# Retention's values and gates and the sparse keys and values: projected by seven block products ahead of the attention, and handed over through DRAM

## The chip, the cores and the metric

The kernel is one program on one core of a Trainium2 chip. The metric is the device time in microseconds of one execution, lower is better: the time that the core needs from the start to the end of the program. Everything is float32; TensorE takes its operands as fp32r, in three passes (below).

## The reference, cut to what matters

A decoder trunk of two layers on 512 tokens of width 1024. Each layer is a half SwiGLU block, a mixer and another half SwiGLU block. The mixer normalises `x` to `u`, projects `u` with one matrix `W_in`, splits the columns among four branches and merges the branches under gates:

```python
u = rms_norm(x, mix_norm[l])
(a_q, a_k, a_v, b_x, b_b, b_c,
 c_q, c_kc, c_vc, c_ks, c_vs, c_kw, c_vw, c_g,
 d_q, d_k, d_v, d_g, gate_logits) = jnp.split(u @ w_in[l], SPLIT_POINTS, axis=-1)
y_a = swa_sink_mixer(a_q, a_k, a_v, ...)          # attention in a window of 128
y_b = short_conv_mixer(b_x, b_b, b_c, conv_w[l])
y_c = nsa_mixer(c_q, c_kc, c_vc, c_ks, c_vs, c_kw, c_vw, c_g, ...)
y_d = retention_mixer(d_q, d_k, d_v, d_g, ...)    # silu(gate) * norm(o), o from q, k, v
branch = jnp.einsum('btnw,nwd->btnd', ys, w_branch[l])
merged = jnp.sum(sigmoid(gate_logits + bias) * branch, axis=2)
x = x + merged @ w_out[l]
```

The columns that matter here are three blocks of 512: `d_v` (values of the retention), `d_g` (its gate), and `c_ks, c_vs, c_kw, c_vw` (four blocks of 128: keys and values of the selected and of the windowed attention of branch C; called the sparse keys and values here).

## The kernel before, in words

**A product in three passes.** A factor `x` is split into `hi` (rounded to fp32r, by ScalarE, line 214) and `lo = x - hi` (by VectorE, line 215). A product is `hi*hi + hi*lo + lo*hi`, three matmuls for each tile of 128 rows of the contraction. This split is the work that ScalarE and VectorE do for every weight.

**Seven block products.** The feed-forward blocks and the stage `early` compute a product with a 2x2 block scheme of seven products in place of eight: the contraction (1024) and the 512 tokens are halved, sums of blocks of the weights are formed by VectorE (`sum_t`, line 439), and combinations of the token blocks are kept ready in `Ahi`, `Alo` and `E` (`factor`, line 330). `step` (line 442) makes one such step for 512 columns of weights: seven units `r1, r2, r6, r5, r7, r3, r4`, each of 24 matmuls of 256 columns (`product`, line 426, line 433), with the copies and sums that put the four output blocks into the tile `O`. `step` loads its weights by two transfers of 1 MB (`load_pair`), one step ahead. Output: features on partitions, tokens along the free dimension; the stationary operand is the weight, the moving one the tokens.

**Dense projections.** In the mixer, `proj_fm` (line 763; features on partitions) and `proj_tm` (line 769; tokens on partitions) multiply without the scheme: for 512 columns 96 matmuls of 512 columns (4 token tiles x 8 rows of the contraction x 3 passes), lines 232 and 782. `proj_tm` leaves its result in four PSUM tiles.

**The order of a layer.** `ffn1`; then `early(l)`: the gates of merge 2 (two steps), the convolution (three steps) and half the gates of merges 1 and 0 (two steps), seven steps in all; gates go to DRAM (`gated`), the convolution too (`yconv`). Then `mixer`: `swa_prep`, `swa`, `merge(1)`, `retention`, `merge(0)`, `nsa`, `merge(3)`, `merge(2)`, the product with `w_out`, and `ffn2`. In `retention` (line 848) four dense projections stand in this order: gates and queries (280 columns), keys (256), values `ps_v` (512), gate `ps_g` (512). The queries and keys are rotated by VectorE (lines 881 to 889, eight operations of 256 elements for each of four token tiles); the gate goes through tanh (line 900) and two VectorE operations of 512 (lines 901, 902). Then a loop over four chunks of 128 tokens: transposes (908), scores (924), mask (925), values (931), state (933, 938, 945), statistics and a reciprocal root (949 to 954), scale (958), gate (959), transposes (962), and `put_y` (840), which splits the result for the merge. In `nsa` the query projection comes first, then `proj_tm(O_KS, 512)` with the compression's products between its halves, then `kv_prep` (line 1012), then the attention.

**What sets the order.** A planner puts each engine's instructions into a fixed order ahead of time: program order is the priority, `tc.high_priority()` lifts an instruction, and what is ready fills the gaps. So the matmuls of a merge (line 232 for its gates, line 828 for its branch product) fill TensorE while the attention written before it waits for VectorE. `tc.issue_after(mark["swa"])` keeps retention's matmuls behind the last value matmul of `swa`; `issue_after(mark["ret"])` keeps those of `nsa` behind retention's last matmul of line 933. SP issues the weight loads in its order, POOL (GpSimd's queue) the loads of gates from DRAM (line 796, two buffers `th`).

Of the kernel before, what the change touches and what calls it, by code (L numbers as in the profile page):

```python
# [13 lines left out]
OP = mybir.AluOpType  # L14
# [58 lines left out]
def body(tc, ins, out):  # L73
# [20 lines left out]
    def fv(ap):  # L94
        return ap.bitcast(F32)
# [157 lines left out]
    def leave(key):  # L253
        ph[key + "_cm"].__exit__(None, None, None)
        ph[key] = None

    def open_x():
        fp = enter("fp", "right")
        ph["XT"] = [fp.tile([128, T], F32, name="XT", tag=f"XT{d}", bufs=1) for d in range(KT)]

    def e_t():
        return cp.tile([128, 2048], F32R, name="E", tag="E", bufs=3)
# [157 lines left out]
        act.activation(t, ps, AF.Copy)  # L420
        return t

    def half(t):
        return t.rearrange("p (w t) -> p w t", w=2)

    def product(ps, w, u, first, last):
# [12 lines left out]
        dve.tensor_tensor(t, a, b, op=OP.add)  # L439
        return t  # L440

    def step(line, raws, srcs, p, use, norm=None, between=([], [])):

        v = {}  # L450

        def blocks(p):
            if p not in raws:
                raws[p] = load_pair(*srcs[p])
            v = raws[p].rearrange("p w (c b) (a n) -> p (w c) b a n", b=2, a=2)
            return [[v[:, :, b, a] for b in range(2)] for a in range(2)]
# [24 lines left out]
        def p4():  # L481
            return unit(v["X"][1][1])

        def r1(w):
            v["x"] = sc_t()
            product(v["x"], w, 0, True, False)
            v["sn1"] = snap(v["x"], "sn1")

        def r2(w):
            py = pv_t()  # L490
            product(py, w, 1, True, True)
            v["O"] = ph["hp"].tile([128, 2048], F32, name="O", tag="O", bufs=2).rearrange("p (w f h t) -> p w f h t", w=2, f=2, h=2)
            dve.tensor_tensor(v["O"][:, :, 0, 0], half(py), half(v["sn1"]), op=OP.add)
# [12 lines left out]
        def r7(w):  # L506
            product(v["x"], w, 4, False, False)
            dve.scalar_tensor_tensor(v["O"][:, :, 1, 1], half(v["x"]), -1.0, half(v["Z"]), op0=OP.mult, op1=OP.subtract)

        def r3(w):  # L510
            product(v["z"], w, 5, False, True)
            dve.tensor_tensor(v["O"][:, :, 0, 1], half(v["z"]), half(v["U"]), op=OP.add)

        def r4(w):
            product(v["x"], w, 6, False, True)
            act.activation(v["O"][:, :, 1, 0], half(v["x"]), AF.Copy, scale=-1.0)
# [12 lines left out]
        line.add(p4, r4)  # L529
# [97 lines left out]
    def early(l):  # L627
# [46 lines left out]
        def gate_cols(b, half_):  # L674
            o = O_MG + b * D + half_ * 512
            return [cols(o), cols(o + 256)]

        for q in range(2):
            srcs.append(gate_cols(2, q))
            uses.append(gates(2, q))  # L680
        for q in range(2):
            srcs.append([cols(O_BX + 256 * q), cols(O_BC + 256 * q)])
            uses.append(conv(2 * q))
# [3 lines left out]
            srcs.append(gate_cols(b, 1))  # L687
            uses.append(gates(b, 1))
        for p in range(len(srcs)):
            step(line, raws, srcs, p, uses[p], norm_end if p == 0 else None)  # L690
        return line


    def mixer(l, spill, F):
# [48 lines left out]
        def w2():  # L743
            return mp.tile([128, 512], F32, name="w2", tag="w2", bufs=6)
# [1 line left out]
        def ks_t():  # L746
            return aq.tile([128, 512], F32, name="ks", tag="ks", bufs=2)

        mark, pv_last, scaled = {}, [None], {}

        def together(first, ready):

# [35 lines left out]
        def merge(b, y, perm, done=None):  # L788
# [2 lines left out]
            gen = weights_fm(w_in, O_MG + b * D, KT if (b, 1) not in slots else KT // 2)  # L791

            def gate(d):
                if (b, d // 4) in slots:
# [45 lines left out]
        def put_y(ps, y, i):  # L840

            ts = slice(i * 128, (i + 1) * 128)
            p = ps.rearrange("p (k t) -> p k t", k=4)
            act.activation(y[0][:, :, ts], p, AF.Copy)
            dve.tensor_tensor(y[1][:, :, ts], p, fv(y[0][:, :, ts]), op=OP.subtract)


        def retention(ps_q, ps_k, ps_v, ps_g):

            yh, yl = y_tiles()  # L850
            o_ = 128 + _CM
# [36 lines left out]
                dve.tensor_tensor(t[:, 0:4], rot[:, 0:4], C["xi"][:, :, None].to_broadcast([128, 4, HD]), op=OP.mult)  # L888
                dve.tensor_tensor(t[:, 4:8], rot[:, 4:8], C["zeta"][:, :, None].to_broadcast([128, 4, HD]), op=OP.mult)
            v = [b4().rearrange("p (i e) -> p i e", i=2) for _ in range(2)]  # L890
            pv = ps_v()
            for i in range(NT):
                act.activation(v[i // 2][:, i % 2], pv[i], AF.Copy, scale=rc[:, i:i + 1])
            g = [b4().rearrange("p (i e) -> p i e", i=2) for _ in range(2)]
            pg = ps_g()
            for i in range(NT):
                x = g[i // 2][:, i % 2]
                act.activation(x, pg[i], AF.Copy, scale=rc[:, i:i + 1])
# [113 lines left out]
        def kv_prep(pk, nt, gains):  # L1012
# [3 lines left out]
            m = 2 * nt  # L1016
            ss = small([128, NT * m], name="kss", bufs=2)
            krs = []
            for i in range(NT):
                src = pk[i][:, :256 * nt].rearrange("p (y w n) -> p y w n", y=nt, w=2)  # L1020
                act.activation(Vt[:, i], src[:, :, 1], AF.Copy, scale=rc[:, i:i + 1])
                kr = w2()[:, :128 * nt].rearrange("p (y n) -> p y n", y=nt)
                act.activation(kr, src[:, :, 0], AF.Copy, scale=rc[:, i:i + 1])
# [173 lines left out]
        def nsa(gates):  # L1197
# [1 line left out]
            cg = compress()  # L1199
            next(cg)  # L1200
            qT, rr = q_prep(O_CQ, lambda: next(cg))
            V, kT = kv_prep(proj_tm(O_KS, 512, lambda: next(cg)), 2, [nk3[:, 1], nk3[:, 2]])
            kcT, vb = next(cg)
            cm = C["cmpm"].rearrange("p (i n) -> p i n", i=NT)
            g3 = gates.rearrange("p i (h b) -> p i h b", b=3)
# [49 lines left out]
        ya = swa(*pa)  # L1255
        merge(1, yb, False)
        with tc.issue_after(mark["swa"].ins):
            yd, gates = retention(lambda: proj_tm(O_CG, 280), lambda: proj_tm(O_DK, 256), lambda: proj_tm(O_DV, 512), lambda: proj_tm(O_DG, 512))
        merge(0, ya, True)
        with tc.issue_after(mark["ret"].ins):  # L1260
            yc = nsa(gates)
# [10 lines left out]
            dve.tensor_tensor(lo, merged[:, d], fv(hi), op=OP.subtract)  # L1272

        leave("mx")
        open_x()
        ph["two"] = True
        merge(2, yc, True, out_in)
        leave("mg")


        XT = ph["XT"]
        line, raws = Line(), {}
        raws[0] = load(ins["w_out"][l][:, :256], KT, 256)
# [55 lines left out]

    slots = {(2, 0): 0, (2, 1): 1, (1, 1): 2, (0, 1): 3}  # L1340
    gated = [xd.tile([128, 2 * KT, T], F32, name="gs", tag=f"gs{l}") for l in range(L)]
    yconv = [xd.tile([128, 2, 4, T], F32, name="yc", tag=f"yc{l}") for l in range(L)]

    def to_mix(l):
# [72 lines left out]
```

## Time and profile before

| | before |
|---|---|
| time, median of 3 runs | 2737.55 us (2736.95 to 2737.64) |
| the profiled execution | 2738.36 us, span 2735.8 us |
| TensorE busy | 2708.0 us, 99% of the span, 17303 matmuls |
| VectorE busy | 2088.2 us, 76% |
| ScalarE busy | 1346.9 us, 49% |
| GpSimd busy | 65.0 us, 2% |
| granted TensorE clock, mean | 0.999 |
| HBM read, written | 269.64 MB, 18.87 MB (105 GB/s over the span) |

The span runs from the first to the last instruction of the program; the execution's own time is 2.56 us longer. A matmul's end is modelled, so that matmuls that follow each other overlap in the busy time; what a run of them costs is read from the chain of waits, where each piece runs to the start of the next. Positions are microseconds from the span's start: layer 0 has `early` at 369 to 511 and the mixer at 511 to 986; layer 1 repeats it 1352 us later (the product with `w_out` begins at 986.51 and at 2338.22 in the chain of waits).

### The profile page before, as it was taken

The numbers are of one execution on the slowest core, as the hardware profiler recorded it, in microseconds if no ns is written. First come the engines' busy times: TensorE is split into PE (matmuls) and PEld (weight loads), VectorE is DVE, ScalarE is ACT, GpSimd is POOL, SyncE is SP. The second block draws the span as 40 slices with busy tenths as digits, with TensorE's granted clock in tenths as the row PEclk, the third lists the DMA queues.
The fourth block names the chain that finished last, engine by engine and source line by source line (L and its number), as shares of the span: only waits on it lengthen the run. The fifth ranks groups of instructions, "written<-read, shape, count | busy, mean of one in ns | idle before, by whom it ended". The sixth has DMA issues, their size and how long they took to land.

```text
span 2735.8 us, 42526 instructions
## 1 busy us (share of the span) xinstructions
PE 2708.0 (99%) x17303; PEld 2368.5 (87%) x17303; DVE 2088.2 (76%) x3474; ACT 1346.9 (49%) x2136; POOL 65.0 (2%) x70
## 2 busy tenths in 40 slices
PE   8999999999999999999999999999999999999999
PEld 7999999978877679999899999998788766899997
DVE  8887899674858679786897868996658586788774
ACT  7444565563336645443554435655532465554442
POOL 0000010000000010000000000000000000100000
PEclk9999999999999999999999999999999999999999
DMA  5223433523232142323323333344233223332322
GB/s 172 93 90 111 131 105 123 190 73 121 84 123 62 50 166 79 122 85 100 124 78 113 96 101 128 110 149 149 82 102 100 101 62 105 112 109 93 114 73 77
DMA packets 243335, 291.24 MB, mean 106 GB/s; under 512 B 8060, under 2 KB 211652, under 8 KB 241092
## 3 DMA queue, kind: packets, MB, share of 16 engines
q1 hardware_dynamic: 235604, 273.78, 30.8%
q0 software_dynamic: 3136, 12.59, 1.4%
q8 instruction: 135, 2.21, 0.3%
q10 hardware_dynamic: 4400, 2.17, 0.3%
q14 instruction: 60, 0.49, 0.1%
HBM read 269.64 MB, written 18.87 MB: 105 GB/s over the span
## 4 chain that ended last, share of the span: by engine, by line
PE 84%; issue 10%; DVE 3%; ACT 2%; DMA 1%; POOL 0%; ACTq 0%; POOLq 0%; DVEq 0%
PE sc L433 23%; PE mm L563 16%; PE tp L433 11%; PE mm L232 7%; PE pv L433 5%; PE mm L828 5%; PE mm L782 3%; PE mm L1300 3%; PE pv L1101 2%; PE tp L1088 2%; PE sc L1050 1%; PE pv L782 1%; PE sc L1051 1%; DVE wlo L215 1%; DMA rawd<-in_ffn_w_down_dram 1%
## 5 line engine op out<-in xcount | busy, mean ns | idle before, releaser
L214 ACT ACTIVATE whi<-raw 128x1024 fp32r<-128x1024 f32 (+2 forms) x338 | 334.0, 989 | 551.3 <-PE mm L563 122.6
L215 DVE TENSOR_TENSOR wlo<-raw,whi 128x1024 fp32r<-128x1024 f32 (+2 forms) x338 | 382.2, 1135 | 173.9 <-ACT whi L214 167.2
L563 PE MATMUL mm<-h,whi 128*128 128x512 f32 x1408 | 443.0, 395 | 0.2 <-DVE h L550 0.2
L214 ACT ACTIVATE whi<-s 128x1024 fp32r<-128x1024 f32 x232 | 245.8, 1060 | 337.6 <-PE tp L433 81.9
L215 DVE TENSOR_TENSOR wlo<-s,whi 128x1024 fp32r<-128x1024 f32 x232 | 282.9, 1221 | 48.0 <-ACT whi L214 47.3
L563 PEld LDWEIGHTS mm<-h,whi 128*128 128x128 f32 x1408 | 260.0, 188 | 59.7 <-DVE h L550 0.6
L433 PE MATMUL sc<-E,whi 128*128 128x256 f32 x1856 | 295.9, 281 | 0.0
L563 PE MATMUL mm<-h,wlo 128*128 128x512 f32 x704 | 277.9, 395 | 0.0
L433 PEld LDWEIGHTS sc<-E,whi 128*128 128x128 f32 x1856 | 253.1, 190 | 0.4 <-ACT sn L420 0.4
L433 PE MATMUL sc<-E,wlo 128*128 128x256 f32 x928 | 186.3, 282 | 0.0
L567 DVE SCALAR_TENSOR_TENSOR XT<-mm,XT 128x512 f32<-128x512 f32 x128 | 88.1, 688 | 125.6 <-PE mm L563 125.5
L433 PE MATMUL sc<-Ahi,whi 128*128 128x256 f32 x816 | 165.3, 283 | 3.3 <-ACT whi L214 3.3
L232 PE MATMUL mm<-Ahi,whi 128*128 128x512 f32 x416 | 165.2, 397 | 0.0
L232 PE MATMUL mm<-Ahi,wlo 128*128 128x512 f32 x416 | 164.7, 396 | 0.0
L433 PE MATMUL sc<-Ahi,wlo 128*128 128x256 f32 x816 | 163.9, 282 | 0.5 <-DVE wlo L215 0.5
L232 PE MATMUL mm<-Alo,whi 128*128 128x512 f32 x416 | 164.1, 394 | 0.0
L433 PE MATMUL sc<-Alo,whi 128*128 128x256 f32 x816 | 163.9, 282 | 0.0
L563 PEld LDWEIGHTS mm<-h,wlo 128*128 128x128 f32 x704 | 132.0, 187 | 32.1
L214 ACT ACTIVATE whi<-rawd 128x1024 fp32r<-128x1024 f32 (+1 forms) x96 | 94.6, 988 | 131.1 <-PE sc L433 66.0
L433 PE MATMUL tp<-E,whi 128*128 128x256 f32 x928 | 148.1, 281 | 0.0
L433 PEld LDWEIGHTS sc<-E,wlo 128*128 128x128 f32 x928 | 143.4, 190 | 0.2 <-DVE wlo L215 0.2
L439 DVE TENSOR_TENSOR s<-s,raw 128x1024 f32<-128x1024 f32 x116 | 141.6, 1221 | 0.9
(318 smaller groups left out, 6041.5 us busy)
## 6 DMA issues: line engine op xcount, KB each, us to landing
raw<-in_w_in_dram SPq DMA_DIRECT2D x66, 1024.0 KB, 6.0
raw<-in_ffn_w_gate_dram SPq DMA_DIRECT2D x44, 1024.0 KB, 5.2
raw<-in_ffn_w_up_dram SPq DMA_DIRECT2D x44, 1024.0 KB, 7.8
rawd<-in_ffn_w_down_dram SPq DMA_DIRECT2D x32, 1024.0 KB, 5.2
rawd<-in_ffn_w_down_dram SPq DMA_DIRECT2D x16, 768.0 KB, 4.3
gs<-O SPq DMA_DIRECT2D x8, 1024.0 KB, 4.0
raw<-in_w_branch_dram SPq DMA_DIRECT2D x8, 1024.0 KB, 7.5
th<-gs POOLq DMA_DIRECT2D x32, 256.0 KB, 3.2
```

Source lines behind the costliest of these rows:

```text
L214: act.activation(hi, src, AF.Copy)
L215: dve.tensor_tensor(lo, src, fv(hi), op=OP.subtract)
L232: pe.matmul(ps, x, y, start=first and j == 0, stop=last and j == len(passes) - 1)
L433: pe.matmul(ps[:, g * 256:(g + 1) * 256], x[:, g * 4 + c], factor(u, s, c), start=first and n == 0, stop=last and n >= 22, skip_group_chec ...
L439: dve.tensor_tensor(t, a, b, op=OP.add)
L563: pe.matmul(ps, x[:, k, j * 128:(j + 1) * 128], h[:, s, b], start=k == 0 and n == 0, stop=k == nf - 1 and n == 2)
L567: dve.scalar_tensor_tensor(XT[d], ps, 0.5, XT[d], op0=OP.mult, op1=OP.add)
L782: pe.matmul(ps[i][:, :n], a, w, start=kk == 0 and j == 0, stop=kk == KT - 1 and j == 2)
L828: pe.matmul(ps, x[:, k], v[:, k], start=k == 0 and j == 0, stop=k == 3 and j == 2)
L1088: t = pe.transpose(ps[:, r * 128:(r + 1) * 128], P[4 * g + r][:, j * 128:(j + 1) * 128], ident)
L1101: pv_last[0] = pe.matmul(pv[g * 64:(g + 1) * 64], V(g, j), pts[g], start=first and j == 0, stop=last and j == nblk - 1)
L1300: pe.matmul(ps, x[:, k], v, start=k == 0 and j == 0, stop=k == KT - 1 and j == 2)
```

## The change

`early` gets three more steps, between the gates of merge 2 and the convolution, with `tm=True`: in them `product_tm` exchanges the operands' roles, so that the result has tokens on partitions. The token factor is stationary (128 tokens at a time), the weights move, 256 columns as two runs of 128. Each step's result is scaled by the norm's factor on ScalarE (four operations of 512) and written to DRAM as `tmaj[l][:, k]` (1 MB). `retention` and `kv_prep` no longer project: they load `tmaj` by POOL's queue (retention four loads of 512 KB, `kv_prep` eight of 128 KB in runs of 512 bytes). The three `proj_tm` of 512 columns and their copies out of PSUM are gone. Beside this: `put_y` of the last token tile gets high priority, and the gates of merge 2 are loaded ahead into the eight tiles that `XT` takes afterwards, so the reload of `XT` from `spill` comes after merge 2.

```diff
+    def product_tm(ps, w, u, first, last):
+        whi, wlo = (t.rearrange("p (g c) n -> p c g n", g=2) for t in w)
+        n = 0
+        for c in st["order"]:
+            for x, s in ((whi, 0), (whi, 1), (wlo, 0)):
+                for i in range(2):
+                    pe.matmul(ps[:, i * 256:(i + 1) * 256], factor(u, s, c)[:, i * 128:(i + 1) * 128], x[:, c], start=first and n == 0,
+                              stop=last and n >= 22, skip_group_check=True)
+                    n += 1
-    def step(line, raws, srcs, p, use, norm=None, between=([], [])):
+    def step(line, raws, srcs, p, use, norm=None, between=([], []), tm=False):
+        product = product_tm if tm else product_fm
...
+        def tokens(k):
+            def use(O):
+                z = O.rearrange("p h i w f n -> p (h i) (w f n)")
+                for i in range(NT):
+                    act.activation(z[:, i], z[:, i], AF.Copy, scale=st["rc"][:, i:i + 1])
+                sp.dma_start(tmaj[l][:, k], z)
+            return use
...
+        for k, o in enumerate((O_DV, O_DG, O_KS)):
+            srcs.append([cols(o), cols(o + 256)])
+            uses.append(tokens(k))
...
             ts = slice(i * 128, (i + 1) * 128)
             p = ps.rearrange("p (k t) -> p k t", k=4)
-            act.activation(y[0][:, :, ts], p, AF.Copy)
-            dve.tensor_tensor(y[1][:, :, ts], p, fv(y[0][:, :, ts]), op=OP.subtract)
+            with tc.high_priority() if i == NT - 1 else ExitStack():
+                act.activation(y[0][:, :, ts], p, AF.Copy)
+                dve.tensor_tensor(y[1][:, :, ts], p, fv(y[0][:, :, ts]), op=OP.subtract)
...
             v = [b4().rearrange("p (i e) -> p i e", i=2) for _ in range(2)]
-            pv = ps_v()
-            for i in range(NT):
-                act.activation(v[i // 2][:, i % 2], pv[i], AF.Copy, scale=rc[:, i:i + 1])
+            for q in range(2):
+                pool.dma_start(v[q], tmaj[l][:, 0, 2 * q:2 * q + 2])
             g = [b4().rearrange("p (i e) -> p i e", i=2) for _ in range(2)]
-            pg = ps_g()
+            for q in range(2):
+                pool.dma_start(g[q], tmaj[l][:, 1, 2 * q:2 * q + 2])
...
+            if pk is None:
+                kv = tmaj[l][:, 2].rearrange("p i (y w n) -> p i y w n", y=nt, w=2)
+                krt = [p_t().rearrange("p (i y n) -> p i y n", i=2, y=nt) for _ in range(2)]
+                for i in range(NT):
+                    pool.dma_start(krt[i // 2][:, i % 2], kv[:, i, :, 0])
+                for i in range(NT):
+                    pool.dma_start(Vt[:, i], kv[:, i, :, 1])
...
-            V, kT = kv_prep(proj_tm(O_KS, 512, lambda: next(cg)), 2, [nk3[:, 1], nk3[:, 2]])
+            next(cg)
+            next(cg)
+            V, kT = kv_prep(None, 2, [nk3[:, 1], nk3[:, 2]])
...
         leave("mx")
-        open_x()
+        enter("fp", "right")
         ph["two"] = True
+        for d in range(KT):
+            ahead[2, d] = x_t(d)
+            pool.dma_start(ahead[2, d], gated[l][:, slots[2, d // 4] * 4 + d % 4])
         merge(2, yc, True, out_in)
         leave("mg")
+        open_x()
```

## Rows read from the trace of the kernel before

**Rows 1.** The page: TensorE's busy time and share of the span.
```profile
PE 2708.0 (99%) x17303; PEld 2368.5 (87%) x17303; DVE 2088.2 (76%) x3474; ACT 1346.9 (49%) x2136; POOL 65.0 (2%) x70
```

**Rows 2.** Waits of TensorE: us in total, times, longest.
```profile
PE mm L828 <- ACT E L844: 2.8, 2, 1.4
PE tp L1036 <- DVE ks L1010: 1.6, 4, 0.5
PE mm L828 <- DVE y L845: 1.3, 2, 0.6
```

**Rows 3.** The chain of waits, layer 0, early and the first projection: start, us, what.
```profile
387.14 5.72 PE sc L433 x48
...
511.38 21.80 PE mm L232 x96
```

**Rows 4.** The chain of waits, layer 0, retention's value and gate projections.
```profile
647.62 4.08 PE mm L782 x18
651.70 1.36 PE pv L782 x6
```

**Rows 5.** Windows: stretch, length, busy us of PE, PEld, DVE, ACT, POOL, clock, DMA.
```profile
389.00:409.00 20.00, 19.59 (x165) 19.39 (x164) 19.43 (x28) 12.32 (x17) 0.00 (x0) 1.00 0.29 99
...
618.00:641.40 23.40, 23.40 (x189) 23.36 (x188) 6.83 (x10) 8.91 (x18) 0.00 (x0) 1.00 0.36 128
641.40:685.50 44.10, 44.10 (x199) 36.59 (x198) 22.87 (x45) 15.70 (x20) 0.00 (x0) 1.00 0.43 122
685.50:737.00 51.50, 51.33 (x300) 41.54 (x299) 42.42 (x127) 16.69 (x26) 1.08 (x2) 1.00 0.19 60
```

**Rows 6.** VectorE's groups in one gate step of early, 389 to 409.
```profile
L215 DVE TENSOR_TENSOR wlo<-s,whi 128x1024 fp32r<-128x1024 f32 x4 | 4.9, 1220 | 0.0
...
L215 DVE TENSOR_TENSOR wlo<-raw,whi 128x1024 fp32r<-128x1024 f32 x3 | 3.7, 1219 | 0.2 <-ACT whi L214 0.2
...
L642 DVE TENSOR_TENSOR O<-O,R 128x2048 f32<-128x2048 f32 x1 | 2.3, 2286 | 0.0
```

**Rows 7.** VectorE's groups, 641.4 to 656.5: one of eight like it, the rotation.
```profile
L882 DVE TENSOR_TENSOR b<-b,P 128x256 f32<-128x256 f32 x4 | 1.7, 420 | 0.0
```

**Rows 8.** Timeline of VectorE, layer 0: a gate operation, and the loop's first mask.
```profile
685.13 0.69 DVE L902 TENSOR_TENSOR b<-b,P 128x512 f32<-128x512 f32 x1
...
689.01 0.76 DVE L925 TENSOR_TENSOR w<-sc,P 128x256 f32<-128x256 f32 x2
```

**Rows 9.** The chain of waits, layer 0: retention's last matmul of line 933, and after.
```profile
736.93 0.22 PE pv L933 x2
737.15 9.24 PE mm L828 x40
```

**Rows 10.** VectorE's groups in the chunk loop, 685.5 to 737: the `lo` operations.
```profile
L215 DVE TENSOR_TENSOR wlo<-raw,whi 128x1024 fp32r<-128x1024 f32 (+1 forms) x9 | 8.9, 986 | 1.7 <-PE mm L232 1.6
```

**Rows 11.** The chain of waits at the end of nsa, layer 0.
```profile
958.68 1.14 PE mm L828 x4
...
959.84 1.06 ACT whi L214
```

**Rows 12.** Windows at the end of nsa, layer 0, columns as in Rows 5.
```profile
960.00:962.80 2.80, 0.78 (x3) 0.30 (x2) 2.66 (x4) 1.38 (x2) 0.00 (x0) 1.00 0.74 256
963.40:966.90 3.50, 3.50 (x10) 2.74 (x9) 0.68 (x1) 0.00 (x0) 0.54 (x1) 0.52 1.11 361
```

**Rows 13.** DMA issues: out<-in, count, KB each, median us to landing.
```profile
th<-gs POOLq DMA_DIRECT2D x32, 256.0 KB, 3.2
...
E<-yc POOLq DMA_DIRECT2D x4, 1024.0 KB, 7.2
```

**Rows 14.** Timeline, layer 0: one VectorE operation without and with an issue by POOL.
```profile
941.12 1.67 DVE L1079 TENSOR_SCALAR P<-P,w 128x512 f32<-128x512 f32 x4
...
946.51 0.73 POOL L796 DMA_DIRECT2D th<-gs  x1 [203.27 <-DVE w L1075]
...
946.64 1.67 DVE L1079 TENSOR_SCALAR P<-P,w 128x512 f32<-128x512 f32 x4
```

More of the change, by code (lines that the diff above doesn't have):

```diff
@@ L255, in leave, with x_t @@
         ph[key] = None
+    def x_t(d):
+        return ph["fp"].tile([128, T], F32, name="XT", tag=f"XT{d}", bufs=1)
     def open_x():
-        fp = enter("fp", "right")
-        ph["XT"] = [fp.tile([128, T], F32, name="XT", tag=f"XT{d}", bufs=1) for d in range(KT)]
+        if ph.get("fp") is None:
+            enter("fp", "right")
+        ph["XT"] = [x_t(d) for d in range(KT)]
     def e_t():
@@ L421, in snap, with product_fm @@
         return t
-    def half(t):
-        return t.rearrange("p (w t) -> p w t", w=2)
-    def product(ps, w, u, first, last):
+    def product_fm(ps, w, u, first, last):
         whi, wlo = w
@@ L440, in sum_t, with half, block @@
         return t
-    def step(line, raws, srcs, p, use, norm=None, between=([], [])):
-        v = {}
+    def product_tm(ps, w, u, first, last):
[8 more added lines that the diff above has]
+    def step(line, raws, srcs, p, use, norm=None, between=([], []), tm=False):
+        v = {}
+        product = product_tm if tm else product_fm
+        def half(t):
+            return t.rearrange("p (i w n) -> p i w n", i=2, w=2) if tm else t.rearrange("p (w t) -> p w t", w=2)
+        def block(a, h):
+            return v["O"][:, h, :, :, a] if tm else v["O"][:, :, a, h]
         def blocks(p):
@@ L491, in r2 @@
             product(py, w, 1, True, True)
-            v["O"] = ph["hp"].tile([128, 2048], F32, name="O", tag="O", bufs=2).rearrange("p (w f h t) -> p w f h t", w=2, f=2, h=2)
-            dve.tensor_tensor(v["O"][:, :, 0, 0], half(py), half(v["sn1"]), op=OP.add)
+            O = ph["hp"].tile([128, 2048], F32, name="O", tag="O", bufs=2)
+            v["O"] = O.rearrange("p (h i w f n) -> p h i w f n", h=2, i=2, w=2, f=2) if tm else O.rearrange("p (w f h t) -> p w f h t", w=2, f=2, h=2)
+            dve.tensor_tensor(block(0, 0), half(py), half(v["sn1"]), op=OP.add)
         def r6(w):
@@ L507, in r7 @@
             product(v["x"], w, 4, False, False)
-            dve.scalar_tensor_tensor(v["O"][:, :, 1, 1], half(v["x"]), -1.0, half(v["Z"]), op0=OP.mult, op1=OP.subtract)
+            dve.scalar_tensor_tensor(block(1, 1), half(v["x"]), -1.0, half(v["Z"]), op0=OP.mult, op1=OP.subtract)
         def r3(w):
             product(v["z"], w, 5, False, True)
-            dve.tensor_tensor(v["O"][:, :, 0, 1], half(v["z"]), half(v["U"]), op=OP.add)
+            dve.tensor_tensor(block(0, 1), half(v["z"]), half(v["U"]), op=OP.add)
         def r4(w):
             product(v["x"], w, 6, False, True)
-            act.activation(v["O"][:, :, 1, 0], half(v["x"]), AF.Copy, scale=-1.0)
+            act.activation(block(1, 0), half(v["x"]), AF.Copy, scale=-1.0)
             use(v["O"])
@@ L680, in early @@
             uses.append(gates(2, q))
+        ntm = len(srcs), len(srcs) + 3
+        for k, o in enumerate((O_DV, O_DG, O_KS)):
+            srcs.append([cols(o), cols(o + 256)])
+            uses.append(tokens(k))
         for q in range(2):
@@ L689, in early @@
         for p in range(len(srcs)):
-            step(line, raws, srcs, p, uses[p], norm_end if p == 0 else None)
+            step(line, raws, srcs, p, uses[p], norm_end if p == 0 else None, tm=ntm[0] <= p < ntm[1])
         return line
@@ L747, in ks_t @@
             return aq.tile([128, 512], F32, name="ks", tag="ks", bufs=2)
-        mark, pv_last, scaled = {}, [None], {}
+        mark, pv_last, scaled, ahead = {}, [None], {}, {}
         def together(first, ready):
@@ L793, in gate @@
             def gate(d):
+                if (b, d) in ahead:
+                    return ahead[b, d]
                 if (b, d // 4) in slots:
@@ L843, in put_y, with retention @@
             p = ps.rearrange("p (k t) -> p k t", k=4)
-            act.activation(y[0][:, :, ts], p, AF.Copy)
-            dve.tensor_tensor(y[1][:, :, ts], p, fv(y[0][:, :, ts]), op=OP.subtract)
-        def retention(ps_q, ps_k, ps_v, ps_g):
+            with tc.high_priority() if i == NT - 1 else ExitStack():
+                act.activation(y[0][:, :, ts], p, AF.Copy)
+                dve.tensor_tensor(y[1][:, :, ts], p, fv(y[0][:, :, ts]), op=OP.subtract)
+        def retention(ps_q, ps_k):
             yh, yl = y_tiles()
@@ L890, in retention @@
             v = [b4().rearrange("p (i e) -> p i e", i=2) for _ in range(2)]
-            pv = ps_v()
-            for i in range(NT):
-                act.activation(v[i // 2][:, i % 2], pv[i], AF.Copy, scale=rc[:, i:i + 1])
+            for q in range(2):
+                pool.dma_start(v[q], tmaj[l][:, 0, 2 * q:2 * q + 2])
             g = [b4().rearrange("p (i e) -> p i e", i=2) for _ in range(2)]
-            pg = ps_g()
+            for q in range(2):
+                pool.dma_start(g[q], tmaj[l][:, 1, 2 * q:2 * q + 2])
             for i in range(NT):
                 x = g[i // 2][:, i % 2]
-                act.activation(x, pg[i], AF.Copy, scale=rc[:, i:i + 1])
                 t = w2()
@@ L1018, in kv_prep @@
             krs = []
-            for i in range(NT):
[L1020 to L1023, printed above, removed]
+            if pk is None:
[5 more added lines that the diff above has]
+                    pool.dma_start(Vt[:, i], kv[:, i, :, 1])
+            for i in range(NT):
+                if pk is None:
+                    kr = krt[i // 2][:, i % 2]
+                else:
+                    src = pk[i][:, :256 * nt].rearrange("p (y w n) -> p y w n", y=nt, w=2)
+                    act.activation(Vt[:, i], src[:, :, 1], AF.Copy, scale=rc[:, i:i + 1])
+                    kr = w2()[:, :128 * nt].rearrange("p (y n) -> p y n", y=nt)
+                    act.activation(kr, src[:, :, 0], AF.Copy, scale=rc[:, i:i + 1])
                 sq = w2()[:, :128 * nt].rearrange("p (y n) -> p y n", y=nt)
@@ L1257, in mixer @@
         with tc.issue_after(mark["swa"].ins):
-            yd, gates = retention(lambda: proj_tm(O_CG, 280), lambda: proj_tm(O_DK, 256), lambda: proj_tm(O_DV, 512), lambda: proj_tm(O_DG, 512))
+            yd, gates = retention(lambda: proj_tm(O_CG, 280), lambda: proj_tm(O_DK, 256))
         merge(0, ya, True)
@@ L1274, in mixer @@
         leave("mx")
-        open_x()
+        enter("fp", "right")
         ph["two"] = True
+        for d in range(KT):
+            ahead[2, d] = x_t(d)
+            pool.dma_start(ahead[2, d], gated[l][:, slots[2, d // 4] * 4 + d % 4])
         merge(2, yc, True, out_in)
         leave("mg")
+        open_x()
         XT = ph["XT"]
@@ L1341, in body @@
     gated = [xd.tile([128, 2 * KT, T], F32, name="gs", tag=f"gs{l}") for l in range(L)]
+    tmaj = [xd.tile([128, 3, NT, T], F32, name="tm", tag=f"tm{l}") for l in range(L)]
     yconv = [xd.tile([128, 2, 4, T], F32, name="yc", tag=f"yc{l}") for l in range(L)]
```

## The prediction

> **What bounds the kernel now.** I read the page first: TensorE is busy for 99% of the span [rows 1]. That alone does not make it the bound, because ends of matmuls are modelled, so I read next what it waited for: the waits of the mixer are the two on `put_y`, 2.8 and 1.3 us over both layers, 1.6 us at `kv_prep`'s transposes [rows 2], and less. Then the chain of waits gives the real pace: in `early` 48 matmuls of 256 columns take 5.72 us, one unit of 24 so 2.86 us [rows 3]; in the dense projections 18 + 6 matmuls of 512 columns take 4.08 + 1.36 = 5.44 us [rows 4]. TensorE is the bound nearly everywhere, and time changes by the matmul work removed, unless the removal leaves it without work. So the second view is windows around retention: while the value and gate projections run (641.4 to 685.5), VectorE is busy for 22.87 of 44.1 us; in the chunk loop behind them (685.5 to 737) for 42.42 of 51.5 [rows 5]. There VectorE comes close, and the change takes the matmuls away exactly ahead of that loop.
>
> **The matmuls.** A projection of 512 columns is four pieces of 5.44 us: 21.76 us; the three removed are 65.3 us per layer. A step of `early` is seven units of 2.86: 20.0 us; the three added are 60.1. Gain 5.2 us per layer, **10.4 us** in all. One thing the trace does not show: in `product_tm` the moving operand comes as two runs of 128 columns with a gap; all moving operands of before are one run. Below, a gain is excluded: as many columns stream. Above, if each run cost what a matmul of 128 columns costs (line 933: 0.22 us for two [rows 9]), 504 matmuls would cost 0.22 in place of 0.119 us each, 51 us per layer. The nearest reading of runs with gaps is VectorE's: `lo` from `raw` (runs of 128) takes 1219 ns and from the unbroken `s` 1220 [rows 6]. I take nothing, and keep the other end as a rival.
>
> **Early's other engines.** A token step needs 7 `lo` and 4 sums of 1024 elements at 1.22 us (sums are of the same size and form) and three output operations of 512 at 0.69 [rows 6, 8]: 13.4 + 2.1 = 15.5 us of VectorE in 20.0. A gate step needs 2.3 us more for its scaling [rows 6], and even the one that also holds the norm's small operations (VectorE 19.43 of 20) kept TensorE busy for 19.59 [rows 5]. ScalarE does seven copies and four operations of 512 as a gate step does, 12.32 of 20. SP gets six loads of 1 MB in place of six of 1 MB, and three stores of 1 MB behind their step's scaling, as the gates have them; behind each waits the load for the step after, a step ahead of its use. Cost nothing; if that cover went, a unit would wait for one `lo`, 1.2 us.
>
> **Retention.** Here lies the doubt. The end of the key projection at 641.4 stays the start. The rotation is 32 operations of 0.42 us [rows 7], 13.4 us on VectorE, with two `lo` of 1.2 us between: until 657.2. Before, this stood under the value projection; now only merge 0 can stand there. The gate's eight operations of 0.69 [rows 8], 5.5 us, can move ahead to 618 to 641, where VectorE is busy for 6.83 of 23.4 us [rows 5], if its loads are in: four on POOL of 512 KB, each between the 3.2 us of 256 KB and the 7.2 us of 1 MB [rows 13]. The loop from the first mask (689.01) to the last matmul of line 933 (737.15) took 48.1 us [rows 8, 9]. In it VectorE did for merge 0 8.9 us of `lo` [rows 10] and three kinds of four operations of 512 (lines 801, 832, 833) at 0.69 [rows 8]: 17.2 us. Since 15.8 us of merge 0's matmuls will be spent before the loop, some of these go too; bounds for the loop are 48.1 (nothing gone) and 30.9 (all gone), and I take 45, near the row. The last matmul of line 933 then comes at 657.2 + 45 = 702.2. TensorE's work for this stretch is what it did from 685.5 to 737.15, 51.6 us, and the rest of merge 0, 9.24 us [rows 9], since `nsa` may not start before that matmul: 60.9 us, until 702.3. So the two just meet. Bounds of idle time: none, or 8.5 us (first rival). A fixed order seldom packs two full engines, so I take a sixth of that, 1.5 us per layer: **3.0 us** lost. Layer 1 repeats the pattern.
>
> **The end of `nsa`.** The last `put_y` waits: merge 3's matmuls end at 959.82, one `hi` copy on ScalarE stands ahead of it at 959.84 [rows 11], TensorE idles for 2.0 of 2.8 us and then has 3.5 us at 0.52 of its clock, so at the lower level of 1.2 GHz [rows 12]. With priority the copy can follow the value matmuls that end at 958.68, under merge 3's last matmuls. The waits are 4.1 us in all [rows 2]; half a microsecond per layer may stay, so **3.1 us** gained. Bounds: nothing (if ScalarE has begun a copy of 1.06 us) and 5.8 (with the 1.7 us that the half clock took, once in the two layers; I leave these out).
>
> **`kv_prep`.** Its products were counted; its copies from PSUM become eight loads on POOL. One behind the other at 3.2 us [rows 13] they take 26 us, under six query and compression tiles of 24 matmuls, 32.7 us [rows 3], even if they start only when retention frees its buffers. Behind them in POOL's queue stand merge 3's and merge 2's gates, needed later still. Nothing; if not covered, up to one load, 3 us per layer.
>
> **Gates of merge 2 ahead, `XT` later.** Eight loads move into free tiles; the reloads of `XT` wait for merge 2 on SP, and behind them stand `w_out`'s loads. Tile 0 is free after an eighth of merge 2, and each unit of `w_out`, 24 matmuls, gives 5.4 us more. Nothing; uncovered at most one load of 3.2 us.
>
> **A rule against it.** POOL issues twelve more loads per layer. An operation of VectorE in four pieces took 1.67 us when POOL was silent and the same 1.67 when POOL issued beside it for 0.73 us [rows 14]: so nothing is counted. The Trainium skill (GPSIMD Engine Reference, Key points) says that GpSimd shares its SBUF interfaces with VectorE and that they contend when VectorE uses both ports; by it each issue could hold VectorE for 0.73 us, and with retention's four inside the loop the sum would be 5.8 us worse, 2733. The trace does not bear it out.
>
> **Sum.** -10.4 + 3.0 - 3.1 = -10.5 us on the profiled execution: 2738.36 (span 2735.8 and 2.56 around it) to 2727.9. That execution lies 0.8 us above the median 2737.55, so on the median's scale 2727.
>
> **Rivals.**
> *A, retention starves (slower).* The gate's loads come late, its 5.5 us fall behind the rotation, and the loop keeps its 48.1 us: first mask near 662.7, last matmul of line 933 at 710.8, TensorE out of work at 702.3. Idle 8.5 us, and a half-clock stretch of 1.7 us as after the idle time of [rows 12]: 10.2 per layer. -10.4 - 3.1 + 20.4 = +6.9: 2744. For it: VectorE's 42.42 of 51.5. Against: some of merge 0's VectorE work goes ahead. It makes the change even at 6.8 us per layer, slower by 0.2% from 9.5.
> *B, about half of it.* `put_y` still finds ScalarE in a copy (0) and retention idles for 4 us per layer: -10.4 + 8 = -2.4: 2735.
> *C, no loss and all of the end.* No idle time in retention, both waits and the half clock gone, and the 1.6 us of waits before `kv_prep`'s transposes [rows 2] gone too: -10.4 - 5.8 - 1.6 = -17.8: 2720.
> *D, the runs with gaps are slow.* Up to 2 x 51 us more: about 2828.
>
> **Chances.** Forecast 0.50 (its own range 2722 to 2731), B 0.22, A 0.16, C 0.10, D 0.02. The range 2719 to 2742 takes in the forecast, B and C, 0.82; A and D are left out. A run can tell about 0.2% from no change, 5.5 us: faster (forecast, C) 0.60, the same (B) 0.22, slower (A, D) 0.18.
>
> **What would show it.** In the changed profile: a token step in `early` of 20 us with VectorE near 15.5; the two waits of line 828 gone from TensorE's list; no wait of TensorE between the key projection and the last matmul of line 933, which should come about 60 us after it. Wrong would be: idle time of more than 4 us there, or 24 matmuls of a token step that take clearly over 2.86 us.

## The result, and the profile after

The changed kernel takes 2769.8 us (median of four runs, 2768.3 to 2771.2); the kernel before took 2737.6 us beside it. The ratio is 1.0115, with an interval of 1.0102 to 1.0127: slower by 32 us, where I had forecast 10.5 us less. The profiled execution has a span of 2767.6 us, 31.8 more than before. Of the four executions of e4 below, one took 4443.1 us at a mean granted clock of 0.555, and e4's figures leave it out. Lines have moved: the values' matmuls are 965 (first factor) and 967 (state), the mask 959, the scale 992, the gate 993, `put_y`'s transposes 996, the gate's VectorE operations 935 and 936, `kv_prep`'s transposes 1080.

The page, the engines' row [rows 1]:

```profile
PE 2713.5 (98%) x17735; PEld 2394.5 (87%) x17735; DVE 2142.7 (77%) x3534; ACT 1374.9 (50%) x2170; POOL 80.3 (3%) x94
```

TensorE's share is almost what it was, so this row hides the loss: at half clock an engine is busy too. The Trainium skill (Perfetto Trace Analysis, introduction) calls matmul busy time a bad metric, because matmuls are pipelined; here 99% against 98% goes with 32 us.

TensorE's waits (total, times, longest), to hold against [rows 2]:

```profile
PE tp L996 <- DVE w L993: 12.0, 2, 6.1
PE tp L1080 <- DVE ks L1044: 9.0, 4, 4.0
PE pv L965 <- DVE w L959: 7.6, 4, 3.3
...
PE mm L862 <- DVE th L835: 1.2, 3, 0.5
PE tp L948 <- DVE E L880: 1.1, 2, 0.6
```

The two waits at `put_y` are gone. In their place stand retention's third chunk (12.0 us), its first (7.6) and `kv_prep`'s transposes (9.0, before 1.6).

The chain in a token step of `early` [rows 3]:

```profile
427.32 2.88 PE tp L450 x24
430.20 5.72 PE sc L450 x48
```

Windows of the changed kernel, layer 0, columns as in [rows 5]: a token step, then the places where TensorE runs dry, each with what follows.

```profile
429.00:449.00 20.00, 20.00 (x169) 20.00 (x169) 15.14 (x15) 11.82 (x15) 0.00 (x0) 1.00 0.49 168
703.90:719.00 15.10, 15.10 (x74) 11.62 (x73) 15.10 (x40) 5.33 (x10) 0.00 (x0) 1.00 0.30 66
719.00:723.60 4.60, 1.33 (x13) 1.10 (x13) 4.55 (x10) 0.88 (x1) 0.00 (x0) 1.00 0.00 0
723.60:727.00 3.40, 3.16 (x11) 2.49 (x10) 3.37 (x14) 0.72 (x1) 0.00 (x0) 0.50 0.00 0
757.00:766.20 9.20, 9.16 (x47) 7.43 (x47) 7.11 (x25) 1.29 (x2) 0.83 (x2) 1.00 0.58 193
766.20:771.40 5.20, 0.00 (x0) 0.00 (x0) 4.51 (x14) 0.83 (x1) 0.00 (x0) 1.00 0.12 43
771.40:781.60 10.20, 8.26 (x37) 7.07 (x38) 2.82 (x9) 1.58 (x3) 0.00 (x0) 0.50 0.01 2
829.40:832.80 3.40, 2.88 (x12) 2.36 (x12) 3.33 (x12) 1.56 (x6) 0.00 (x0) 0.50 0.13 40
```

From 703.9 on, where the key projection ends, VectorE is busy without a break, and from 719 TensorE waits for it. Each idle stretch is followed by one in which the granted clock is 0.50 of full speed: 3.4 us after the first chunk's gap, 10.2 after the third chunk's, 3.4 at `kv_prep`. Layer 1 has the same three, and longer:

```profile
2088.90:2095.70 6.80, 5.49 (x16) 4.60 (x17) 6.30 (x22) 0.72 (x1) 0.00 (x0) 0.50 0.00 0
2136.70:2150.40 13.70, 9.35 (x39) 7.97 (x40) 6.25 (x22) 1.58 (x3) 0.00 (x0) 0.50 0.00 0
2194.70:2201.60 6.90, 5.24 (x18) 4.17 (x19) 6.13 (x22) 4.23 (x11) 0.00 (x0) 0.51 0.51 162
```

POOL, VectorE and ScalarE (three timelines of layer 0), where the swish of the gate went:

```profile
676.53 1.08 POOL L927 DMA_DIRECT2D b<-tm  x2
677.61 1.05 POOL L930 DMA_DIRECT2D b<-tm  x2
```
```profile
716.19 0.41 DVE L924 TENSOR_TENSOR b<-b,cst 128x256 f32<-128x256 f32 x1
716.52 1.28 DVE L935 SCALAR_TENSOR_TENSOR b<-w,b 128x512 f32<-128x512 f32 x2
...
721.27 1.28 DVE L936 TENSOR_TENSOR b<-b,P 128x512 f32<-128x512 f32 x2
722.48 0.74 DVE L959 TENSOR_TENSOR w<-sc,P 128x256 f32<-128x256 f32 x2
```
```profile
709.81 1.06 ACT L214 ACTIVATE whi<-raw 128x1024 fp32r<-128x1024 f32 x1 [5.01 <-PE mm L232]
713.37 0.63 ACT L214 ACTIVATE whi<-raw 128x512 fp32r<-128x512 f32 x1 [2.50 <-PE mm L862]
713.91 2.18 ACT L934 ACTIVATE w<-b 128x512 f32<-128x512 f32 x4
```

The loads are issued by 678.7 (such a load lands after 6.7 us, median), but the tanh stands at 713.9 in ScalarE's order, with ScalarE idle for 5.0 and 2.5 us just ahead, and VectorE's eight operations stand behind the whole rotation, directly ahead of the first mask.

**The books.** Of the change of +31.8 us in span: matmuls -10.4; the waits at `put_y` and the half clock behind one -5.8 [rows 2, 12]; new waits in retention 12.0 + 7.6 + 1.1 = +20.7; at `kv_prep` 9.0 - 1.6 = +7.4; at half clock 44.4 us, of which at most half is lost, +22.2. That is +34.1, 2.3 too much; some of the waits lie inside half-clock stretches and count twice. The profiled execution also has 13.7 us at half clock at its start (13.6 to 27.3), which that of the kernel before has not. The same gate step of `early` begins at 388.53 in place of 387.14 [rows 3], so at most 1.4 us of the change come from there, and the books leave it out.

### The profile page after: what moved, and what is told of

Its sections match the earlier page's. It is cut to its first block, busy times and chain, and to the rows that moved or that the text cites. A ratio compares the mean times of both kernels' runs of the same rounds, so it can differ in the third digit from the quotient of the medians.

```text
span 2767.6 us, 43594 instructions
## 1 busy us (share of the span) xinstructions
PE 2713.5 (98%) x17735; PEld 2394.5 (87%) x17735; DVE 2142.7 (77%) x3534; ACT 1374.9 (50%) x2170; POOL 80.3 (3%) x94
## 4 chain that ended last, share of the span: by engine, by line
PE 91%; DVE 4%; ACT 2%; issue 1%; DMA 1%; ACTq 0%; POOL 0%; DVEq 0%; POOLq 0%
PE sc L434 24%; PE mm L583 16%; PE tp L434 12%; PE mm L232 10%; PE pv L434 6%; PE mm L862 5%; PE mm L1351 3%; PE sc L450 2%; PE pv L1145 2%; PE mm L814 2%; PE tp L1132 2%; PE sc L1094 1%; PE tp L450 1%; DVE wlo L215 1%; PE sc L1095 1%
## 5 line engine op out<-in xcount | busy, mean ns | idle before, releaser
L214 ACT ACTIVATE whi<-raw 128x1024 fp32r<-128x1024 f32 (+2 forms) x332 | 327.3, 987 | 494.2 <-PE mm L583 122.9
L215 DVE TENSOR_TENSOR wlo<-raw,whi 128x1024 fp32r<-128x1024 f32 (+2 forms) x332 | 374.2, 1133 | 114.4 <-ACT whi L214 104.8
L214 ACT ACTIVATE whi<-s 128x1024 fp32r<-128x1024 f32 x256 | 271.3, 1060 | 359.9 <-PE tp L434 83.6
L215 DVE TENSOR_TENSOR wlo<-s,whi 128x1024 fp32r<-128x1024 f32 x256 | 312.0, 1220 | 60.0 <-ACT whi L214 59.5
L583 PEld LDWEIGHTS mm<-h,whi 128*128 128x128 f32 x1408 | 259.9, 188 | 60.3 <-DVE h L570 1.3
L440 DVE TENSOR_TENSOR s<-s,raw 128x1024 f32<-128x1024 f32 x128 | 156.2, 1220 | 1.3
L440 DVE TENSOR_TENSOR s<-raw 128x1024 f32<-128x1024 f32 x128 | 156.1, 1220 | 1.2
```

Source lines behind the costliest of these rows:

```text
L214: act.activation(hi, src, AF.Copy)
L215: dve.tensor_tensor(lo, src, fv(hi), op=OP.subtract)
L583: pe.matmul(ps, x[:, k, j * 128:(j + 1) * 128], h[:, s, b], start=k == 0 and n == 0, stop=k == nf - 1 and n == 2)
```

## The experiments

Theory 1: the removed projections were TensorE's cover while VectorE rotates, gates and masks; without them TensorE waits, and pays again in clock. Rivals: the hand-over through DRAM and POOL's queue; merge 0's gate loads; the side edits. Medians below are compared with the changed kernel's 2769.8 and with the kernel before, which took 2738.3 to 2738.7 beside these runs.

**e1, the side edits alone.** The kernel before, with `put_y`'s priority, merge 2's gates ahead, `XT` later.

> The kernel before with the side edits alone: put_y of the last token tile at high priority, the gates of merge 2 loaded ahead, XT later; nothing goes through DRAM. If the loss of 32 us comes from the projections that left retention (theory 1), these edits only gain: the two waits at put_y, 4.1 us, and perhaps the half clock behind one, 1.7 us: 2732 to 2734 us. If the side edits are what costs (rival), it is slower than the kernel before: above 2740 us.

2732.1 us, ratio 0.9978 (0.9969 to 0.9987). The rival falls. The gain of 6.4 us is about the two waits and the half clock together. What follows is held against it; less the matmuls' 10.4, 2722 would be the change without any loss.

**e2 and e3, the hand-overs apart.**
```diff
-        for k, o in enumerate((O_DV, O_DG, O_KS)):
+        for k, o in ((2, O_KS),):              # e2;  e3: ((0, O_DV), (1, O_DG))
...
```

> Only the sparse keys and values go through early and DRAM; retention's values and gate are projected densely again. Matmuls: two token steps for two dense projections, 2 x (20.03 - 21.76) = -3.5 us; the put_y waits -4.1. Theory 1 (retention starves when its two projections are gone): retention's 16 us per layer are not lost, only what kv_prep's transposes wait, up to 2.7 us per layer: 2730 to 2736 us. Rival (what costs is the hand-over itself, through DRAM and POOL's queue, in every one of the three): a third of the 32 us lost plus the gains, about 2745 us or more.

> Only retention's values and gate go through early and DRAM; the sparse keys and values are projected densely in nsa again, as before. Theory 1: nearly the whole loss stays, 2765 to 2771 us. Rival (each of the three hand-overs costs its share): about 2759 us.

2742.0 and 2760.0 us. Over e1 that is +9.9 and +27.9; 2732.1 + 9.9 + 27.9 = 2769.9, so the parts add up to the changed kernel. Both numbers lie nearer to the rival's than to mine: `kv_prep` loses more than I said. TensorE's waits of e2, where retention is as before:

```profile
PE tp L1081 <- DVE ks L1045: 9.0, 4, 4.0
```

and ScalarE's squares of the keys there, with VectorE's first scale, two timelines:

```profile
806.07 1.32 ACT L1070 ACTIVATE w<-P 128x256 f32<-128x256 f32 x4
```
```profile
812.71 1.07 DVE L1041 SCALAR_TENSOR_TENSOR w<-P,rs_y,gt 128x64 f32<-128x64 f32 x5
```

The squares read the keys, whose four loads had been issued by 634.8 (the load of 773.3, which the expectation of e6 names, is one of the values'). In ScalarE's order they stand behind the query projection's copies, and the dense projection that used to follow there is gone.

**e4, cover put back in front of the loop.**
```diff
+            for _ in range(2):
+                ps = mm_t()
+                for j in range(24):
+                    pe.matmul(ps, A[0][:, j % 8, 0:128], A[1][:, j % 8], start=j == 0, stop=j == 23)
+                act.activation(w2(), ps, AF.Copy)
             S = p_t().rearrange("p (h c) -> p h c", h=RH)
```

> The changed kernel with 48 matmuls of 512 columns more per layer on factors that lie in SBUF, right behind the key projection, two PSUM tiles whose copies nobody uses: 10.9 us of TensorE work per layer, 21.8 us in all, and two copies of 512 on ScalarE. Theory 1 says that TensorE stands idle or at half clock in retention for about 16 us per layer: the added work fills that, and the time stays or falls, 2755 to 2772 us, with fewer half-clock stretches in retention. Rival (the time goes elsewhere, in transfers or in queues behind them): the added work adds itself, 2769.8 + 21.8 = about 2791 us.

2778.8 us (2778.3 to 2786.3 in three runs): neither, and nearer to the theory. The 21.8 us of added work cost 9.0 (8.5 to 16.5 by the run), so about 13 lay in gaps. Its waits (retention's third chunk, the merge, the first chunk's mask; lines are five higher):

```profile
PE tp L1001 <- DVE w L998: 9.5, 2, 4.9
...
PE mm L862 <- DVE vv L992: 5.9, 2, 2.9
...
PE pv L970 <- DVE w L964: 1.0, 2, 0.5
```

The first chunk's wait is filled (7.6 to 1.0) and the half clock behind it is gone. The third chunk's wait is smaller by 2.5 us only, with 10.2 us at half clock behind it in each layer, and a wait at line 862 (2.9 us in each layer) is new: cover ahead of the loop does little for a gap at its end.

**e5, the gate ahead of the rotation.** The loads of `g`, the tanh and lines 935 and 936 are moved up behind the key projection's copies.

> The changed kernel with the gate's loads, tanh and eight VectorE operations written ahead of the rotation, so that their 5.5 us stand where my forecast had put them. If the order of VectorE's work is what starves TensorE at the first chunk (theory 1a), the first mask comes 5 to 6 us earlier, the waits at line 965 (7.6 us) and the half clock behind them (3.4 + 6.8 us long, half of it lost) go: about -12 us, 2757. If only the sum of VectorE's work counts (rival), what is gained at the first chunk comes back at the third: 2767 to 2771.

2754.5 us, -15.3. The gate ran at 696.0 to 701.5, the first mask at 715.28 (722.48 before the move), and TensorE's wait there fell from 7.6 to 1.0:

```profile
PE tp L996 <- DVE w L993: 8.2, 2, 4.1
...
PE pv L965 <- DVE w L959: 1.0, 2, 0.5
```

The order of VectorE's and ScalarE's work is worth about half of the 32 us. The third chunk's wait stays, with 10.2 us at half clock behind it in each layer.

**e6, the K half of `kv_prep` ahead of the query projection.**

> The changed kernel with the K half of kv_prep (loads, squares, reciprocal root) written ahead of nsa's query projection, the rest behind it as it was. The squares ran at 806 us in the run with only the sparse keys through DRAM though POOL had issued the last load at 773. If it is the order (theory 1b), the waits at the transposes (9.0 us) and the half clock behind them (3.4 + 6.8 us long, half of it lost) go: about -14 us, 2756. If the loads land too late (rival), the squares wait for them and it stays at 2767 to 2772.

2764.3 us, -5.6. The squares now run at 775.5 to 780.7, so the loads were there; the waits fall from 9.0 to 4.3 us, and a half-clock stretch of 3.4 us stays in each layer. Order is about half of this place too, though the gain is well under the expected 14. A new wait of 2.0 us, at line 232 for a `hi` copy of ScalarE, takes some of it back. The other half may be that only short matmuls (the compression's, line 1195 of the changed kernel) stand between the last projection and the transposes; no run tests that.

**e7, merge 0's gates loaded ahead.** At the third chunk a gate's load stands in the chain of waits:

```profile
764.73 2.93 DMA th<-gs
767.76 0.69 DVE th L866
768.51 1.14 DVE wlo L215
769.65 1.28 DVE w L992 x4
```
```diff
+        for d in range(4, KT):
+            ahead[0, d] = p_t()
+            pool.dma_start(ahead[0, d], gated[l][:, slots[0, 1] * 4 + d - 4])
         merge(0, ya, True)
```

> The changed kernel with the four gates of merge 0 that come from DRAM loaded ahead into four free tiles P, in place of two buffers th one by one. At the third chunk VectorE waits for such a load (issued 764.73, landed 767.66) with the chunk's scale and gate queued behind it. If that load is the cause (theory 2), the waits at line 996 (12.0 us) and the half clock behind them (10.2 + 13.7 us long, half of it lost) go: about -24 us, 2746. If VectorE's chain itself is late there (theory 1), under 6 us: 2764 or more.

2771.1 us, no gain, though that load is out of the chain and the waits at line 996 fall from 12.0 to 9.5. VectorE then does merge 0's operations without waiting, and they still stand ahead of the chunk's scale:

```profile
770.25 0.69 DVE L867 TENSOR_TENSOR merged<-merged,P 128x512 f32<-128x512 f32 x1
770.86 1.22 DVE L215 TENSOR_TENSOR wlo<-raw,whi 128x1024 fp32r<-128x1024 f32 x1
772.00 1.36 DVE L992 TENSOR_SCALAR w<-pv,mv,rs_y 128x128 f32<-128x128 f32 x4
773.39 0.69 DVE L993 TENSOR_TENSOR w<-w,b 128x512 f32<-128x512 f32 x1
```

The load was the last of several things that were late together; theory 2 falls.

**e8, the three together.**

> The three together: gate ahead of the rotation, K half of kv_prep ahead, gates of merge 0 loaded ahead. If these three places hold the loss and their gains add: -12 - 14 - 24 gives 2720 us; the floor is the run with the side edits alone less the matmuls' 10.4, 2732.1 - 10.4 = 2722. If the missing cover itself decides (VectorE's work in retention is longer than TensorE's in any order), at most the kv_prep part and a few us are gained: 2750 or more.

2750.3 us, -19.5, the sum of the single gains (-15.3 - 5.6 + 1.3). Order alone does not bring it back: the third chunk still waits, 7.6 us over both layers.

**e9, more work for TensorE at the end of the loop.** `nsa`'s compression and query projections no longer wait for retention's last matmul.
```diff
-        with tc.issue_after(mark["ret"].ins):
-            yc = nsa(gates)
+        ng = nsa(gates)          # yields ahead of kv_prep
+        next(ng)
+        with tc.issue_after(mark["ret"].ins):
+            yc = next(ng)
```

> The changed kernel with nsa's compression and query projections freed from waiting for retention's last value matmul; only what is behind them still waits for it. If at the third chunk TensorE waits because merge 0 is used up (missing cover), these projections fill the gap: the waits at line 996 (12.0 us) and the half clock behind them (10.2 + 13.7 us long, half of it lost) go for the most part, 2748 to 2754 us. If VectorE is the bound there, the added work brings its own lo operations in front of the chunk's chain and the gap stays: 2765 or more.

2752.1 us, -17.7, as expected of missing cover. The waits at line 996 fall from 12.0 to 5.2, and no half clock follows them:

```profile
PE tp L1080 <- DVE ks L1044: 9.2, 4, 4.1
PE pv L965 <- DVE w L959: 6.5, 2, 3.3
...
PE tp L996 <- DVE w L993: 5.2, 4, 1.7
```
```profile
757.00:780.00 23.00, 22.21 (x122) 18.14 (x121) 18.97 (x51) 4.42 (x6) 0.57 (x2) 1.00 0.25 84
```

VectorE has more to do in that stretch, 18.97 of 23 us, and the loop is hardly shorter: 57.3 us from the first mask (721.2) to the last matmul of line 967 (778.5), against 58.4. What changed is that TensorE has matmuls beside it and keeps its clock.

**e10, gate and K half ahead, projections freed.**

> The changed kernel with the gate ahead of the rotation, nsa's compression and query projections freed, and the K half of kv_prep ahead. If gains add: 2769.8 - 15.3 (measured for the gate) - 5.6 (measured for the K half) - 8.2 of waits at line 996 and some 8 to 10 us of half clock behind them = 2731 to 2733 us, below the kernel before by 0.2%. If VectorE bounds the stretch: as the run of three edits, 2750.

2735.1 us, ratio 0.9987 (0.9978 to 0.9996), 2 us above my range; no half clock is left in either mixer, and of the waits 4.3 us at `kv_prep` and 3.6 at line 996. It is still 13 above the 2722 of a change without loss; these waits explain some 8 of them and a new one at line 232, for a `hi` copy, 1.6; the rest stays open.

**e11, only the values through DRAM.**

> Only retention's values go through early and DRAM; its gate and the sparse keys and values are projected densely. Half of retention's cover stays, 21.8 us per layer behind the rotation. If half is enough: the run with the side edits alone less 2 x 1.73 us of matmuls, 2732.1 - 3.5 = 2729 us. If every us of cover that goes costs in proportion: half of what values and gate cost together, (2760 - 2732) / 2, above it: 2746 us.

2729.7 us, ratio 0.9966 (0.9953 to 0.9979): the fastest run, below both kernels. Its interval overlaps that of e1, so the 2.4 us between them show that nothing is lost, not how much is gained. One dense projection behind the keys is enough cover for the rotation and the gate: up to the loop's end (736.2) TensorE has next to no wait, at full clock.

```profile
618.00:740.00 122.00, 121.70 (x701) 101.69 (x701) 83.21 (x227) 42.98 (x74) 4.29 (x8) 1.00 0.38 116
```

With this the rival of e2 and e3, one price for each hand-over, falls: the values' costs nothing over e1, the gate's behind it 30 us.

**e12, values and gate, with e5's and e9's edits.**

> Retention's values and gate through early and DRAM, the sparse keys and values dense, the gate ahead of the rotation, nsa's compression (its first part) and query projections freed. From the run with values and gate alone, 2760: - 15.3 for the gate, - 16 to 18 for the waits at the third chunk and their half clock: 2727 to 2729 us. If VectorE bounds the stretch: 2744 or more.

2733.2 us, ratio 0.9981 (0.9971 to 0.9990), 4 us above my range, where e3 took 2760.0: order and cover give back 27 of its 28 us over e1. The two matmul savings are still not to be seen: 4.6 us of waits remain at line 996, and a half clock of 3.4 us in one layer.

**e13, only the gate through DRAM.**

> Only retention's gate goes through early and DRAM; its values and the sparse keys and values are projected densely. With the values alone moved the time was 2729.7 us, with values and gate 2760.0: the second costs 30 us. If that is the cover (either dense projection behind the keys is enough for the rotation and the gate), the gate alone gives what the values alone gave, 2727 to 2732 us. If it is the gate's own hand-over (its eight VectorE operations fall behind the rotation whatever covers it), 2744 or more.

2736.2 us, ratio 0.9990 (0.9980 to 0.9999), between the two. TensorE's cover is there, but the gate is late again: its loads were issued by 637.4, and ScalarE does the tanh behind the values' last copy.

```profile
684.78 0.67 ACT L928 ACTIVATE b<-pv,rc 128x512 f32<-128x512 f32 x1
685.35 2.18 ACT L935 ACTIVATE w<-b 128x512 f32<-128x512 f32 x4
```

VectorE had idled for 3.6 and 3.8 us in the ten before. At the first chunk TensorE does not wait for this; it waits at the last chunk's mask, 1.8 us in layer 0 (at 744.4) and 1.9 in layer 1, with 3.4 us at half clock behind each:

```profile
PE pv L966 <- DVE w L960: 3.7, 2, 1.9
```

That is 3.7 and up to 3.4 us, about the 6.5 by which e13 lies above e11. I put it down to the gate's place in the order, but no run moves the gate alone here, so that is not shown. Nor can the 30 us be split into order and cover: where both were missing, mending the order gave back 15.3 (e5) and mending the cover at the loop's end 17.7 (e9), and with the gate as the first to move, it costs 4.1 over e1 and the values behind it 23.8.

**e14, values and sparse keys, K half ahead, projections freed.**

> Retention's values and the sparse keys and values through early and DRAM, the gate dense; the K half of kv_prep ahead and nsa's compression and query projections freed. If covers add up place by place: 2729.7 (values alone) - 3.5 of matmuls + what the sparse keys still cost with their K half ahead, 13.4 - 5.6 = 7.8 beyond their matmuls: 2734 us; if the freed projections cover that too, 2726 to 2729, below both kernels.

2732.5 us, ratio 0.9978 (0.9968 to 0.9987), near the sum of 2734. The waits at `kv_prep` are 4.3 us and one half clock of 3.4 us stays; against e11 no gain shows from the sparse keys' hand-over.

## Why the prediction was wrong, point by point

- **The matmuls and `early`: right.** 24 matmuls of a token step take 2.84 to 2.88 us (forecast 2.86), so runs with gaps cost nothing and D is out; the three steps add 60.3 us (60.1); VectorE is busy for 15.1 of 20 (15.5).
- **`put_y`: right, and too small.** Both waits went; e1 gives 6.4 us where I took 3.1, a little over my upper bound of 5.8.
- **Retention: the step that failed** is "the gate's eight operations ... can move ahead to 618 to 641" and, built on it, "so the two just meet". The loads were early enough. A fixed order, in which program order is priority, put tanh and gate behind the rotation (which itself ended at 716.6, 2.3 us sooner than forecast), and with them the first mask at 722.5 in place of 657.2 + 61.7 = 718.9; 61.7 is the mixer's shift by `early` (its first projection begins at 573.1). TensorE's side came out near by luck: I had it out of work at 702.3 + 61.7 = 764.0, and it was at 766.2, but it had stood still for 3.3 us and lost up to 1.7 by the clock before that, and the last chunk's matmuls, done by 780.9, were still to come. VectorE's side failed outright: I cut the loop from 48.1 to 45 us, since some of merge 0's VectorE work would go ahead. I had let TensorE do the rest of merge 0 in this stretch, but not VectorE the operations that belong to it. From the first mask to the last matmul of line 967 it took 58.4 us (columns as in [rows 5]; the loop of the kernel before is the first line):

```profile
689.00:737.20 48.20, 48.03 (x273) 39.28 (x274) 38.94 (x122) 14.24 (x21) 1.08 (x2) 1.00 0.20 65
722.50:780.90 58.40, 50.40 (x259) 40.89 (x260) 42.35 (x128) 13.64 (x20) 2.17 (x4) 0.89 0.28 90
```

Lines 866 and 867 of merge 0 run eight times each in it, where their like ran four times each before, and they stand in front of the chunk's chain (e7). That makes VectorE's work longer by 3.4 us; the rest of the ten is engines that wait for each other and half clock, and no run takes these apart. With one dense projection left (e11), the loop took 48.0 us.
- **The price of idle time: missing.** I took 1.5 us of idle time per layer and named 8.5 as the bound; it was 20.7 over both layers, so 10.4 per layer. The larger omission is the clock. Behind these waits lie 34.1 us at half clock, up to 17 us lost; rival A had 1.7 us per layer. A was the nearest mechanism, with the gate behind the rotation and the loop uncut, but the gate was late by its place and not by its loads, the loop grew past 48.1, and A's price was 10.2 us per layer where the runs showed up to 18.9 (10.4 idle, 8.5 of clock).
- **`kv_prep`: wrong.** I took nothing, and at most one late load. No load of the keys was late (e6). The dense projection was itself the cover of VectorE's key scaling, and I counted it only as work: 7.4 us of waits more, and up to 5 of half clock.
- **Gates of merge 2, `XT`:** no cost shows in e1.
- **The rule on POOL's and VectorE's shared interfaces:** VectorE's operations of 512 at 764.39 and 765.10, beside POOL's issue at 764.73, took 0.68 and 0.69 us, as in [rows 8]. The trace still does not bear it out.

## What to carry to other kernels

Before taking matmuls away, ask which engine works under them and how much of its chain then lies bare: the same hand-over cost nothing for the first of two projections (e11) and 30 us for the second; in the other order it was 4 and 24 (e13), so what counts most is whether one of the two stays. Where an order is fixed ahead of time, data that arrive early are used early only if the instruction is written early. An idle stretch of TensorE can be priced twice, once as a wait and once in the clock that follows it, and its busy share shows little of either (99% and 98% here).

## What the runs showed of the hardware

The clock followed the idle stretches closely. With waits of 6.1 and 5.9 us at line 996 the granted clock was 0.50, the lower level of 1.2 GHz, for 10.2 and 13.7 us, and a pair of 128-column matmuls at lines 965 and 967 took 0.43 us in place of 0.22. The Trainium skill (TensorE: Matmul & The Clock Gate, Part 1) says that the clock is set by how busy TensorE was of late, and the rows agree: each of the six half-clock stretches in the changed kernel's mixers begins in or right behind a wait of 3.3 us or more. What I had not expected is how small a gap suffices and that its size alone does not decide. In e13 waits of 1.8 and 1.9 us each had 3.4 us at half clock behind them. In e12 the two waits after the loop, at line 996, were 2.08 and 2.04 us, and only the first was followed by half clock. The longest wait at line 996 in e10, 1.8 us, and one of 2.2 us at line 814 in e7 had none.
